# Five input chunks of 512 columns in place of seven, with other spacings between the parts of attention

## The chip, the core and the metric

The kernel runs on one NeuronCore of a Trainium2 chip. The metric is the device time of one launch in microseconds; three runs of the kernel before gave 290.32, 290.36 and 291.07, median 290.36. TensorE (PE in the profile) multiplies, VectorE (DVE), ScalarE (ACT) and GpSimd (POOL) work elementwise, and SyncE (SP) starts the loads.

## The reference

Two layers of a hybrid attention block on 256 tokens of width 1024. Each layer normalizes x, projects it to ten groups of columns, runs three kinds of attention with a gate on each, and adds the output projection to x:

```python
def hybrid_layer(x, mem, norm_g, w_in, w_out, mem_norm_g, w_mem_kv, qk_g):
    h = rms_norm(x, norm_g)
    proj = jnp.einsum('btd,de->bte', h, w_in)
    ...
    a_q, a_k, a_v, a_g, b_q, b_k, b_v, b_g, m_q, m_g = jnp.split(proj, cuts, axis=-1)
    qa = rope(rms_norm(to_heads(a_q, N_HEADS_MOBA), qk_g[0]))
    ...
    oa = from_heads(moba_attention(qa, ka, to_heads(a_v, N_HEADS_MOBA)))
    ...
    ob = from_heads(dilated_attention(qb, kb, to_heads(b_v, N_HEADS_DIL)))
    ...
    om = from_heads(memory_attention(qm, km, to_heads(m_v, N_HEADS_MEM)))
    y = jnp.concatenate([oa * jax.nn.silu(a_g), ob * jax.nn.silu(b_g), om * jax.nn.silu(m_g)], axis=-1)
    return x + jnp.einsum('bte,ed->btd', y, w_out)
```

The groups aq, ak, av, ag, bq, bk, bv and bg have 384 columns each (six heads of 64), mq and mg 256 (four heads). Queries and keys get a norm for each head, those of a and b a rotation as well. With 256 tokens the a heads are causal attention, the b heads causal attention with a fixed bias for each distance, and the m heads look at a second input, mem, without a mask.

## The kernel before

Weights come from memory in units of up to 1 MB and are cut into a high and a low part: ScalarE casts `hi` (L467), VectorE subtracts to `lo` (L468). Normalized x stands transposed as `xmh` and `xml`, cut in the same way, and each product is three matmuls: high by high, low by high, high by low. TensorE thus has three matmuls for each of the 8 slices k of the width and each of 2 row tiles of 128 tokens.

A layer goes through its columns in chunks. For queries, keys and values a chunk is a projection with x as the weights of the array and the chunk's columns moving (`project`), into two accumulators, one PSUM bank for each row tile. In before the chunks are mkv (512, from mem), mq (256), then bq, bk, bv, aq, ak, av with 384 columns each. The gates mg, bg0, bg1, ag0, ag1 are computed transposed with 256 tokens moving (`project_t`), whatever their width. There are four accumulator banks (`acc`), so a chunk's second accumulator waits until the last reader of an earlier chunk is through: the norms of queries and keys (`normed`, VectorE with help of ScalarE and GpSimd) or, for a gate, a tanh `th` on ScalarE and a product `gate` on VectorE (`gates`).

Attention goes by pairs of heads, numbered by the 128 rows of the output that they make: e = 0 to 2 are the a heads, 3 to 5 the b heads, 6 and 7 the m heads. A pair is a Python generator (`pair_of_heads`): four transposes of queries and keys into a bank `wk` (there are three), a copy `qkT` by ScalarE, scores, a maximum `nm` on VectorE, an exponential and a normalization on ScalarE (`pr`), transposes of the probabilities, a copy `pT` on ScalarE, products with the values (`o<-pT,v`), and the gated result `y` on VectorE, which ScalarE casts to the high part of `yT` and VectorE subtracts to its low part.

TensorE works through its instructions in the order in which the program was written out. That order is made by a clock in the program text: `mm` advances `clock[0]` by what a matmul should take, and after each step of a chunk `poll` runs the generators that have become due. A generator says with `yield D_...` how far behind the present step its next one shall stand. So the constants D_* on top of the file place the parts of attention among the products of the chunks; `finish` advances the clock until a pair is through. A queue on another engine has its own order, the one that a scheduler gave the instructions, and is also worked through from first to last.

The output projection takes the rows of `yT` in the order e = 6, 7, 3, 4, 5, 0 into four banks; e = 1 and 2 come last, by bank: three banks for e = 1, the same for e = 2, then the fourth bank for both.

Of the kernel before, what the change touches and what calls it, by code (L numbers as in the profile page):

```python
# [16 lines left out]
P = 128  # L17
T = 256
# [9 lines left out]
PR_BUFS = 3  # L28
# [39 lines left out]
def hybrid_kernel(ctx: ExitStack, tc: tile.TileContext, x, mem, mem_t, gains, w_in, w_out, w_mem_kv, qk_g, const, out):  # L68
# [26 lines left out]
    mem_sb = cp.tile([P, NT, D], F32, name="mem_sb")  # L95
# [174 lines left out]
    def normed(accs, n, dsts, tables, scale=None):  # L270

        h = n // HD
        half = dict(s=2, d=HD // 2)
        held = []
        for t, acc in enumerate(accs):
# [3 lines left out]
            first = tables[0][t][:, None, :].to_broadcast([P, h, HD])  # L279
            if scale is None:  # L280
                pin(nc.vector.tensor_tensor(heads(t1), heads(acc), first, op=ALU.mult))
            else:
                pin(nc.vector.scalar_tensor_tensor(heads(t1), heads(acc), scale, first, op0=ALU.mult, op1=ALU.mult))
            if len(tables) > 1:
                pin(nc.vector.tensor_tensor(t2.rearrange("p (h s d) -> p h s d", **half),
                                            acc.rearrange("p (h s d) -> p h s d", **half)[:, :, ::-1, :],
                                            tables[1][t].rearrange("p (s d) -> p s d", s=2)[:, None]
                                            .to_broadcast([P, h, 2, HD // 2]), op=ALU.mult))
            held.append((t1, t2, rs))

        def rest():
            for (t1, t2, rs), dst in zip(held, dsts):
                if len(tables) > 1:
                    pin(nc.vector.tensor_tensor(t1, t1, t2, op=ALU.add))
                pin(nc.vector.tensor_tensor(heads(dst), heads(t1), rs.unsqueeze(2).to_broadcast([P, h, HD]),
                                            op=ALU.mult))
# [3 lines left out]
    live = dict(pr=0, pT=0, o=0, heads=0, pairs=0, s=0, t=0, v=0)  # L300

    def pair_of_heads(qn, kn, pair, masks, v, gate, ready, finished, alone):
# [10 lines left out]
        yield from until(lambda: live["s"] == me and live["pr"] + 2 <= PR_BUFS)  # L313
# [3 lines left out]
        live["pr"] += 2  # L317
        scores = [work() for _ in range(2)]
# [8 lines left out]
        for j in range(2):  # L327
            rest = head(2 * me + j, scores[j], spans, masks, pTs, D_SOFTMAX - 1.5 * alone)
            spawn(rest, next(rest))
        yield D_SOFTMAX - 1.5 * alone  # L330
# [409 lines left out]
```

## Time and profile before

| | us |
|---|---|
| median of three runs | 290.36 |
| profiled execution | 289.94 |
| its span, first to last instruction | 288.1 |
| outside the span | 1.84 |
| TensorE busy (98%) | 282.3 |
| VectorE busy (71%) | 205.9 |
| ScalarE busy (69%) | 199.0 |
| GpSimd busy (19%) | 53.4 |
| mean granted clock of TensorE | 1.000 (2.4 GHz) |

A share of busy time close to 100% says that an engine hardly stands, not that it works at its peak. What bounds a kernel is read from the chain of work that ended last and from the waits on it. A row of a timeline gives the start from the span's beginning, the time for which the group of equal instructions lasted, how many there were (x; here one matmul of single precision is sometimes two records) and, in brackets, how long the engine had stood before and what it waited for.

### The profile page before, as it was taken

What the parts mean: (1) busy time and instruction counts of PE and PEld (TensorE: products, weight loads), DVE (VectorE), ACT (ScalarE), POOL (GpSimd) and SP (SyncE); (2) the same over time, 40 slices, a digit from 0 to 9 for tenths busy, and PEclk for the clock granted to TensorE, in tenths of its full rate; (3) what the DMA queues carried; (4) which work ended last, traced back from release to release, by engine and by line L of the source; (5) the groups of instructions that cost most, each with busy time, mean ns of one, the idle gap of its engine ahead of it and who ended that gap; (6) DMA issues with size and microseconds to landing.
All of it is one profiled execution on the core that took longest, in us unless ns stands there. A gap on an engine that the chain in (4) does not pass through costs nothing.

```text
span 288.1 us, 4967 instructions
## 1 busy us (share of the span) xinstructions
PE 282.3 (98%) x1810; PEld 250.5 (87%) x1810; DVE 205.9 (71%) x461; ACT 199.0 (69%) x446; POOL 53.4 (19%) x72
## 2 busy tenths in 40 slices
PE   6999999999999999999999999999999999999994
PEld 5799999898989998777788999989898989897773
DVE  1798999794659987754686576979755899655423
ACT  3899678877678779688267554868685778777620
POOL 0103993200003300000020079403000312000000
PEclk9999999999999999999999999999999999999999
DMA  7999675527430656528024918360845443820003
GB/s 246 390 367 369 207 220 161 170 55 273 111 109 17 206 171 262 190 109 290 1 91 168 275 54 236 131 175 9 281 115 154 146 132 96 361 73 0 3 0 146
DMA packets 32793, 47.33 MB, mean 164 GB/s; under 512 B 1280, under 2 KB 27648, under 8 KB 32768
## 3 DMA queue, kind: packets, MB, share of 16 engines
q1 hardware_dynamic: 32336, 46.22, 48.7%
q10 hardware_dynamic: 432, 0.79, 0.9%
q8 instruction: 14, 0.23, 0.3%
q14 instruction: 11, 0.09, 0.1%
HBM read 45.96 MB, written 1.05 MB: 163 GB/s over the span
## 4 chain that ended last, share of the span: by engine, by line
PE 97%; DMA 1%; DVE 0%; SPq 0%; DVEq 0%; issue 0%
PE acc L111 79%; PE wk L114 8%; PE wk L111 5%; PE o L111 5%; DMA memT<-in_mem_t_dram 1%; PE o L114 0%; DVE x_sb L706 0%; SPq L487 0%; DVE whole L533 0%; DVEq L736 0%; DVEq L533 0%
## 5 line engine op out<-in xcount | busy, mean ns | idle before, releaser
L468 DVE TENSOR_TENSOR lo<-raw,hi 128x768 fp32r<-128x768 f32 (+1 forms) x90 | 95.3, 1087 | 20.4 <-ACT hi L467 19.3
L467 ACT CAST hi<-raw 128x768 fp32r<-128x768 f32 (+1 forms) x90 | 82.5, 937 | 26.8 <-PE acc L111 16.9
L111 PE MATMUL acc<-hi,xmh 128*128 128x384 f32 (+2 forms) x252 | 66.6, 346 | 0.0
L111 PE MATMUL acc<-lo,xmh 128*128 128x384 f32 (+2 forms) x252 | 63.7, 335 | 0.0
L111 PE MATMUL acc<-hi,xml 128*128 128x384 f32 (+2 forms) x252 | 63.6, 334 | 0.0
L156 POOL TENSOR_TENSOR hrs<-ms,mhalf 128x6 f32<-128x6 f32 (+1 forms) x24 | 29.9, 1248 | 116.0 <-DVE ms L155 115.7
L111 PEld LDWEIGHTS acc<-hi,xmh 128*128 128x128 f32 x252 | 43.0, 189 | 4.1 <-issue 2.2
L111 PEld LDWEIGHTS acc<-lo,xmh 128*128 128x128 f32 x252 | 45.0, 188 | 1.1
L111 PEld LDWEIGHTS acc<-hi,xml 128*128 128x128 f32 x252 | 44.9, 188 | 1.1
L111 PE MATMUL acc<-hi,yT 128*128 128x512 f32 x128 | 40.9, 401 | 0.0
L111 PE MATMUL acc<-xmh,hi 128*128 128x256 f32 x128 | 29.7, 293 | 0.0
L378 ACT ACTIVATE pr<-pr,nm 128x128 f32<-128x128 f32 (+1 forms) x48 | 21.3, 445 | 12.0 <-DVE nm L376 12.0
L111 PE MATMUL acc<-xmh,lo 128*128 128x256 f32 x128 | 28.4, 283 | 0.0
L111 PE MATMUL acc<-xml,hi 128*128 128x256 f32 x128 | 28.3, 283 | 0.0
L111 PEld LDWEIGHTS acc<-hi,yT 128*128 128x128 f32 x128 | 23.0, 188 | 4.8 <-issue 0.7
L384 ACT ACTIVATE pr<-pr,rinv 128x128 f32<-128x128 f32 (+1 forms) x64 | 25.5, 461 | 0.0
L111 PE MATMUL acc<-lo,yT 128*128 128x512 f32 x64 | 25.1, 391 | 0.0
L111 PEld LDWEIGHTS acc<-xml,hi 128*128 128x128 f32 x128 | 21.0, 191 | 0.0
L111 PEld LDWEIGHTS acc<-xmh,lo 128*128 128x128 f32 x128 | 21.0, 191 | 0.0
L111 PEld LDWEIGHTS acc<-xmh,hi 128*128 128x128 f32 x128 | 20.9, 191 | 0.0
L376 DVE CUSTOM_DVE_ANT_0 pr<-wk,cst 128x128 f32<-128x128 f32 (+1 forms) x48 | 14.3, 353 | 8.6 <-PE wk L111 8.3
L395 ACT COPY pT<-wk 128x384 f32<-128x384 f32 (+1 forms) x32 | 15.2, 508 | 7.2 <-PE wk L114 7.1
(83 smaller groups left out, 354.6 us busy)
## 6 DMA issues: line engine op xcount, KB each, us to landing
raw<-in_w_in_dram SPq DMA_DIRECT2D x24, 768.0 KB, 5.5
raw<-in_w_in_dram SPq DMA_DIRECT2D x7, 1024.0 KB, 6.6
raw<-in_w_out_dram SPq DMA_DIRECT2D x6, 1024.0 KB, 4.9
raw<-in_w_in_dram SPq DMA_DIRECT2D x6, 512.0 KB, 4.1
raw<-in_w_out_dram SPq DMA_DIRECT2D x4, 512.0 KB, 4.2
raw<-in_w_mem_kv_dram SPq DMA_DIRECT2D x2, 1024.0 KB, 5.7
raw<-in_w_mem_kv_dram SPq DMA_DIRECT2D x2, 512.0 KB, 6.7
x_sb<-in_x_dram SPq DMA_DIRECT2D x2, 512.0 KB, 6.4
```

Source lines behind the costliest of these rows:

```text
L111: pe(nc.tensor.matmul(out, a, b, start=start, stop=stop), us)
L114: pe(nc.tensor.transpose(out, a, ident), 0.109)
L156: pin(nc.gpsimd.tensor_tensor(dst, ms, mhalf[:, :n], op=ALU.pow))
L376: nc.vector.tensor_tensor_reduce(out=pr[:, spans[t]], in0=s[:, spans[t]], in1=masks[t], scale=-1.0, scalar=3e38, op0=ALU.add, op1=ALU.min, ...
L378: nc.scalar.activation(pr[:, spans[t]], pr[:, spans[t]], AF.Exp, scale=-1.0, bias=nm[:, t:t + 1], accum_out=sums[:, t:t + 1])
L384: nc.scalar.activation(pr[:, spans[t]], pr[:, spans[t]], AF.Copy, scale=rinv[:, t:t + 1])
L395: nc.scalar.copy(pT[:, :n], ps[:, :n])
L467: pin(nc.scalar.copy(hi, raw))
L468: pin(nc.vector.tensor_tensor(lo, raw, hi.bitcast(F32), op=ALU.subtract))
```

## The change

Queries, keys and values are cut anew: c0 = mq and the last 256 columns of bv, c1 = bq and the first 128 of bk, c2 = the rest of bk, the first 128 of aq, the first 128 of bv, c3 = the rest of aq and the first 256 of ak, c4 = the rest of ak and av. All have 512 columns, the gates stay. The order of a layer is mkv, c0, mg, c1, c2, bg0, bg1, c3, c4, ag0, ag1 and the output projection. A load of a chunk that consists of several ranges of columns is one DMA for each. `normed` takes the columns in spans that have tables of their own, and queries and keys of a kind stand in a common tile `qk`. The constants of the spacings change, the shorter ones for the last pair (e = 2, `alone`) are dropped, pairs 3, 5 and 7 get longer ones, and there are four buffers of probabilities in place of three. The copy of mem, `mem_sb`, takes the buffer of the first raw weights.

```diff
-PR_BUFS = 3
+PR_BUFS = 4
...
-D_NORM, D_MEM, D_QK, D_SOFTMAX, D_PT, D_EVAC = 8, 1, 2.5, 5, 2.5, 4
+D_NORM, D_WIDE, D_MEM, D_QK, D_SOFTMAX, D_PT, D_EVAC = 8, 9.5, 6.5, 2.5, 5, 2.5, 4
...
-D_PARTNER, D_SCORES = 5, 14
+D_BUSY, D_SCORED = 1.5, 4
+D_PARTNER, D_SCORES = 8, 14
...
-    def normed(accs, n, dsts, tables, scale=None):
+    def normed(accs, n, spans, outs, scale=None):
...
-        yield from until(lambda: live["s"] == me and live["pr"] + 2 <= PR_BUFS)
+        yield from until(lambda: live["s"] == me and live["pr"] + 2 <= PR_BUFS and clock[0] >= live["next"])
...
+        live["next"] = clock[0] + D_SCORED
...
-        yield D_SOFTMAX - 1.5 * alone
+        yield D_SOFTMAX + D_BUSY * busy
         yield from until(lambda: len(pTs) == 2)
-        yield D_PT - alone
+        yield D_PT
...
+    for name, pieces in (("c0", (("mq", 0, 256), ("bv", 128, 384))), ("mg", (("mg", 0, 256),)),
+                         ("c1", (("bq", 0, 512),)), ("c2", (("bk", 128, 384), ("aq", 0, 128), ("bv", 0, 128))),
+                         ("bg0", (("bg", 0, 256),)), ("bg1", (("bg", 256, 384),)),
+                         ("c3", (("aq", 128, 640),)), ("c4", (("ak", 256, 768),)),
+                         ("ag0", (("ag", 0, 256),)), ("ag1", (("ag", 256, 384),))):
+        in_cols[name] = [(first_col[c] + lo, first_col[c] + hi) for c, lo, hi in pieces]
...
-        order += [(l, c) for c in ["mkv", "mq", "mg", "bq", "bk", "bv", "bg0", "bg1", "aq", "ak", "av", "ag0", "ag1", "om", "ob", "oa"]]
+        order += [(l, c) for c in ["mkv", "c0", "mg", "c1", "c2", "bg0", "bg1", "c3", "c4", "ag0", "ag1", "om", "ob", "oa"]]
...
+    mem_sb = sp.tile([P, NT, D], F32, tag="yT0", name="mem_sb", bufs=1)
...
-            ahead[0] = SPLIT_BUFS - 2
+            ahead[0] = SPLIT_BUFS - 1
...
+        accs = run(project(xs, weights(), 512))
+        normed(accs, 512, [span(0, 384, 2), span(384, 512, 3)], [(0, 512, by_tile(qk, 0, 512))])()
+        start_heads(range(1), 3, qn, kn, masks, v, gate, ready, D_WIDE)
+        accs = run(project(xs, weights(), 512))
+        normed([acc[:, 0:384] for acc in accs], 384, [span(0, 256, 3), span(256, 384, 0)],
+               [(0, 256, by_tile(qk, 512, 768)), (256, 384, by_tile(qk_a, 0, 128))])()
+        for t, acc in enumerate(accs):
+            nc.scalar.copy(v[:, t, 0:128], acc[:, 384:512])
+        start_heads(range(1, 3), 3, qn, kn, masks, v, gate, ready)
```

What the constants do is seen in the order of the instructions. The first place is TensorE at the end of layer 1, from the last products with values (pair e = 2) on; `yT` is the gated result, a wait in brackets is on ScalarE's cast or VectorE's subtraction. Before, the pair's two last values products and what follows them (the first wait is for e = 1, the second for e = 2):

```order
L111 MATMUL o<-pT,v 64x128 x2
L111 MATMUL acc<-hi,yT_1952 128x512 [waits Activation_49]
L111 MATMUL acc<-hi,yT_1953 128x512 [waits DVE_49]
L111 MATMUL acc<-lo,yT_1952 128x512
L111 MATMUL acc<-hi,yT_1952 128x512
L111 MATMUL acc<-hi,yT_1953 128x512
L111 MATMUL acc<-lo,yT_1952 128x512
L111 MATMUL acc<-hi,yT_1952 128x512
L111 MATMUL acc<-hi,yT_1953 128x512
L111 MATMUL acc<-lo,yT_1952 128x512
L111 MATMUL acc<-hi,yT_1952 128x512 [waits Activation_49]
L111 MATMUL acc<-hi,yT_1953 128x512 [waits DVE_49]
```

And of the change, the product ahead of them, the values products of e = 2, and what follows (the waits are for e = 2):

```order
L111 MATMUL acc<-hi,yT_1843 128x512
L111 MATMUL acc<-lo,yT_1842 128x512
L111 MATMUL o<-pT,v 64x256 [waits PE_49]
L111 MATMUL o<-pT,v 64x256
L111 MATMUL o<-pT,v 64x128 x2
L111 MATMUL acc<-hi,yT_1842 128x512 [waits Activation_49]
L111 MATMUL acc<-hi,yT_1843 128x512 [waits DVE_49]
L111 MATMUL acc<-lo,yT_1842 128x512
```

The nine products of e = 1 for three banks stood behind the last values, and now stand ahead of them; 24 products follow the values before, 15 now.

The second place is VectorE in layer 0 between mg and the chunk behind it, up to the second gate of mg; t, qn, kn and mqn belong to the norms of the memory heads, hss and ms to the sums of squares. Before:

```order
L295 TENSOR_TENSOR qn<-t_340,hrs 128x256
L295 TENSOR_TENSOR qn<-t_350,hrs 128x256
L632 SCALAR_TENSOR_TENSOR t_392<-v,rmem,gB 128x256
L468 TENSOR_TENSOR lo<-raw,hi 128x768
L635 TENSOR_TENSOR kn<-t_392,hrs 128x256
L632 SCALAR_TENSOR_TENSOR t_395<-v,rmem,gB 128x256
L582 SCALAR_TENSOR_TENSOR gate<-th,acc 128x256
L635 TENSOR_TENSOR kn<-t_395,hrs 128x256
L582 SCALAR_TENSOR_TENSOR gate<-th,acc 128x256
```

Of the change:

```order
L287 SCALAR_TENSOR_TENSOR t_394<-acc,gB 128x256
L262 TENSOR_REDUCE hss<-sq 128x4
L595 SCALAR_TENSOR_TENSOR gate<-th,acc 128x256
L155 TENSOR_SCALAR ms<-hss 128x4
L287 SCALAR_TENSOR_TENSOR t_404<-acc,gB 128x256
L301 TENSOR_TENSOR mqn<-t_394,hrs 128x256
L301 TENSOR_TENSOR mqn<-t_404,hrs 128x256
L480 TENSOR_TENSOR lo<-raw,hi 128x1024
L595 SCALAR_TENSOR_TENSOR gate<-th,acc 128x256
```

The first gate, which frees the bank that the second accumulator of c1 takes, stands ahead of the norm of c0's second row tile; the norm of the memory keys has moved further up, out of these rows.

The third place is ScalarE in layer 0 between the last softmax ahead of ag0's tanh and ag1's tanh (th). Before:

```order
L384 ACTIVATE pr<-pr,rinv 128x128
L384 ACTIVATE pr<-pr,rinv 128x256
L593 CAST yT_257<-y 128x256
L581 ACTIVATE th<-acc 128x256 x2
L467 CAST hi<-raw 128x1024
L395 COPY pT<-wk 128x384
L581 ACTIVATE th<-acc 128x256
L467 CAST hi<-raw 128x1024
L395 COPY pT<-wk 128x384
```

Of the change, from ag0's tanh to ag1's:

```order
L594 ACTIVATE th<-acc 128x256 x2
L386 ACTIVATE pr,sums<-pr,nm 128x128
L316 COPY qkT<-wk 128x512
L386 ACTIVATE pr,sums<-pr,nm 128x256
L386 ACTIVATE pr,sums<-pr,nm 128x128
L392 ACTIVATE pr<-pr,rinv 128x128
L392 ACTIVATE pr<-pr,rinv 128x256
L386 ACTIVATE pr,sums<-pr,nm 128x256
L609 CAST yT_258<-y 128x256
L392 ACTIVATE pr<-pr,rinv 128x128
L392 ACTIVATE pr<-pr,rinv 128x256
L594 ACTIVATE th<-acc 128x256
```

The softmax of a pair (e = 0), with its copy of queries and keys and a cast of `yT`, stands between the two.

## Rows read from the trace of the kernel before

**Rows 1.** page of the profile, busy time of each engine
```profile
PE 282.3 (98%) x1810; PEld 250.5 (87%) x1810; DVE 205.9 (71%) x461; ACT 199.0 (69%) x446; POOL 53.4 (19%) x72
```

**Rows 2.** page of the profile, chain that ended last, by engine
```profile
PE 97%; DMA 1%; DVE 0%; SPq 0%; DVEq 0%; issue 0%
```

**Rows 3.** waits of TensorE, all that the view names
```profile
PE acc L111 <- DVE whole L533: 1.1, 1, 1.1
PE warm L121 <- DVE mhalf L84: 1.0, 1, 1.0
```

**Rows 4.** timeline of TensorE, layer 0, mg to bq (start, duration in us)
```profile
30.33 0.40 PE L111 MATMUL acc<-xmh,lo 128*128 128x256 f32 x2
30.57 0.52 PE L111 MATMUL acc<-hi,xmh 128*128 128x384 f32 x2
...
35.78 0.27 PE L114 MATMUL wk<-ident,qn 128*128 128x128 f32 x1
```

**Rows 5.** timeline of TensorE, end of layer 1
```profile
277.91 0.87 PE L111 MATMUL o<-pT,v 128*64 128x256 f32 x8
278.71 0.74 PE L111 MATMUL acc<-hi,yT 128*128 128x512 f32 x2
...
280.91 0.63 PE L111 MATMUL acc<-hi,yT 128*128 128x512 f32 x2
...
283.64 0.62 PE L111 MATMUL acc<-hi,yT 128*128 128x512 f32 x2
```

**Rows 6.** timeline of ScalarE, layer 0, gates of mg and of bg1
```profile
30.65 0.66 ACT L581 ACTIVATE th<-acc 128x256 f32<-128x256 f32 x2 [0.41 <-PE acc L111]
...
74.48 0.39 ACT L581 ACTIVATE th<-acc 128x256 f32<-128x256 f32 x1
```

**Rows 7.** timeline of VectorE, layer 0, gate of bg1
```profile
74.90 0.42 DVE L582 SCALAR_TENSOR_TENSOR gate<-th,acc 128x256 f32<-128x256 f32 x1 [1.10 <-ACT th L581]
```

**Rows 8.** timeline of VectorE, layer 0, five splits, then norms of a chunk
```profile
59.52 5.22 DVE L468 TENSOR_TENSOR lo<-raw,hi 128x1024 fp32r<-128x1024 f32 x5
...
86.03 0.55 DVE L262 TENSOR_REDUCE hss<-sq 128x6 f32<-128x384 f32 x1
...
90.83 0.95 DVE L468 TENSOR_TENSOR lo<-raw,hi 128x768 fp32r<-128x768 f32 x1
```

**Rows 9.** timeline of TensorE, layer 0, scores to third output bank
```profile
108.47 0.93 PE L111 MATMUL wk<-qkT 64*128 64x128 f32 x8
...
110.13 0.33 PE L114 MATMUL wk<-ident,qn 128*128 128x128 f32 x1
...
119.12 0.62 PE L111 MATMUL acc<-hi,yT 128*128 128x512 f32 x2
```

**Rows 10.** timeline of ScalarE, layer 0, softmax of that pair
```profile
110.34 0.40 ACT L378 ACTIVATE pr<-pr,nm 128x128 f32<-128x128 f32 x1 [0.56 <-DVE nm L376]
...
112.58 1.04 ACT L467 CAST hi<-raw 128x1024 fp32r<-128x1024 f32 x1
113.53 1.49 ACT L384 ACTIVATE pr<-pr,rinv 128x128 f32<-128x128 f32 x4
114.93 0.39 ACT L593 CAST yT<-y 128x256 fp32r<-128x256 f32 x1
```

**Rows 11.** timeline of VectorE, layer 0, first maximum of that pair
```profile
110.02 0.28 DVE L376 CUSTOM_DVE_ANT_0 pr<-wk,cst 128x128 f32<-128x128 f32 x1
```

**Rows 12.** timeline of VectorE, end of layer 1
```profile
278.83 0.42 DVE L359 SCALAR_TENSOR_TENSOR y<-o,gate 128x256 f32<-128x256 f32 x1 [2.29 <-PE o L111]
279.73 0.42 DVE L594 TENSOR_TENSOR yT<-y,yT 128x256 fp32r<-128x256 f32 x1 [0.47 <-ACT yT L593]
```

**Rows 13.** timeline of ScalarE, end of layer 1
```profile
279.29 0.41 ACT L593 CAST yT<-y 128x256 fp32r<-128x256 f32 x1 [3.21 <-DVE y L359]
```

**Rows 14.** timeline of TensorE, transposes of probabilities
```profile
75.32 0.49 PE L114 MATMUL wk<-ident,pr 128*128 128x128 f32 x3
```

**Rows 15.** timeline of ScalarE, copy of those transposes
```profile
75.84 0.48 ACT L395 COPY pT<-wk 128x384 f32<-128x384 f32 x1 [0.26 <-PE wk L114]
```

More of the change, by code (lines that the diff above doesn't have):

```diff
@@ L287, in normed @@
+            for a, b, tables in spans if rotated else ():
+                pin(nc.vector.tensor_tensor(t2[:, a:b].rearrange("p (h s d) -> p h s d", **half),
+                                            acc[:, a:b].rearrange("p (h s d) -> p h s d", **half)[:, :, ::-1, :],
                                             tables[1][t].rearrange("p (s d) -> p s d", s=2)[:, None]
[L288 removed]
+                                            .to_broadcast([P, (b - a) // HD, 2, HD // 2]), op=ALU.mult))
@@ L297, in normed, with pair_of_heads @@
         return rest
     pending = {}
-    live = dict(pr=0, pT=0, o=0, heads=0, pairs=0, s=0, t=0, v=0)
-    def pair_of_heads(qn, kn, pair, masks, v, gate, ready, finished, alone):
+    live = dict(next=0, pr=0, pT=0, o=0, heads=0, pairs=0, s=0, t=0, v=0)
+    def pair_of_heads(qn, kn, pair, masks, v, gate, ready, finished, alone, busy):
         ps = work()
@@ L416, in hybrid_kernel @@
         else:
-            n = 512 if c == "mkv" else in_cols[c][1]
+            n = 512 if c == "mkv" else sum(hi - lo for lo, hi in in_cols[c])
             nk = 8 if n <= 256 else 4
@@ L640, in hybrid_kernel @@
+            if i == 3 and l:
+                normed(keys, 256, [(0, 256, [[gB[:, l, 5]] * NT])], [(0, 256, keys)])()
+        for t, acc in enumerate(accs):
+            pin(nc.scalar.copy(v_b[:, t, 128:384], acc[:, 256:512]))
+        normed([acc[:, 0:256] for acc in accs], 256, [(0, 256, [[gB[:, l, 4]] * NT])], [(0, 256, by_tile(qn, 0, 256))],
+               0.125)()
+        ahead[0] = SPLIT_BUFS - 1
         pinning[0] = False
-        start_heads(2, 6, qn, kn, None, v, gate, ready, D_NORM + D_MEM)
+        start_heads(range(2), 6, qn, kn, None, v, gate, ready, D_MEM)
@@ L642, in hybrid_kernel, with span @@
         tab = prepare_tables(l)
+        def span(a, b, kind):
+            return a, b, [[tab[:, kind, c, t] for t in range(NT)] for c in range(2)]
         gates(run(project_t(xs, weights(), 256)), gate)
@@ new lines, in hybrid_kernel @@
+        for t, acc in enumerate(accs):
+            nc.scalar.copy(v[:, t, 0:128], acc[:, 384:512])
+        start_heads(range(1, 3), 3, qn, kn, masks, v, gate, ready)
+        ready["v"] = clock[0] + D_EVAC
+        gates(run(project_t(xs, weights(), 256)), gate[:, 0:2])
+        gates(run(project_t(xs, weights(), 128)), gate[:, 2:3])
+        masks = [cst[:, C_CAUSAL + 128:C_CAUSAL + 256], cst[:, C_CAUSAL:C_CAUSAL + 256]]
+        if l + 1 < DEPTH:
+            mem_xs = xm_tiles()
+            spawn(next_mem(mem_xs, gT[:, 24 + 8 * l:32 + 8 * l]), D_FIRST_MEM)
@@ new lines, in hybrid_kernel @@
+        (v, gate), qk = head_tiles(384, 384), qk_a
+        qn, kn = qk[:, :, 0:384], qk[:, :, 384:768]
+        ready = dict(v=1e9)
+        accs = run(project(xs, weights(), 512))
+        normed(accs, 512, [span(0, 256, 0), span(256, 512, 1)], [(0, 512, by_tile(qk, 128, 640))])()
+        start_heads(range(2), 0, qn, kn, masks, v, gate, ready, D_WIDE)
+        accs = run(project(xs, weights(), 512))
+        normed([acc[:, 0:128] for acc in accs], 128, [span(0, 128, 1)], [(0, 128, by_tile(qk, 640, 768))])()
@@ L671, in hybrid_kernel @@
+        for t, acc in enumerate(accs):
+            nc.scalar.copy(v[:, t], acc[:, 128:512])
+        start_heads(range(2, 3), 0, qn, kn, masks, v, gate, ready)
+        ready["v"] = clock[0] + D_EVAC
+        gates(run(project_t(xs, weights(), 256)), gate[:, 0:2])
+        gates(run(project_t(xs, weights(), 128)), gate[:, 2:3])
         whole_banks = [(t, c, 512) for t in range(NT) for c in (0, 512)]
```

149 lines of the change are left out of this document (65 added, 84 removed).

## The prediction

> **What bounds the kernel now.** I read the busy shares first, then the chain that ended last, then TensorE's waits, and only then the timelines of the places that the change touches. TensorE is busy for 282.3 of 288.1 us [rows 1], the chain consists of TensorE for 97% of the span [rows 2], and the view of TensorE's waits names one wait of 1.1 us before a product and otherwise only the one before the warming matmuls [rows 3]. So there is no stage in which another engine ends last: the time is the sum of what TensorE issues, and VectorE and ScalarE matter only where a matmul stands behind one of their results. Two things can move the time: how long TensorE takes for its list, and every new wait in that list, which is paid in full.
>
> **What the list itself gains.** The time of a matmul here is its columns plus a fixed part. From the start of the last 256-column group to that of the first 384-column one two matmuls take 0.24 us, 0.120 each; from 30.57 to 35.78 us thirty 384-column matmuls take 5.21, 0.1737 each [rows 4]; at the layer's end twelve 512-column ones take 2.73 us, 0.2275 each [rows 5]. At 2.4 columns per ns the columns alone are 0.1067, 0.160 and 0.2133, so about 13.3 ns stay with each matmul whatever its width. Per k, row tile and product the old chunks need one 256 and six 384, the new ones five 512: the same 2560 columns in two matmuls fewer. With 8 k, 2 row tiles, 3 products and 2 layers that is 96 places and 192 matmuls fewer, 192 x 13.3 ns = **-2.56 us**. TensorE has no cover, so all of it counts, and so does each wait below: all of TensorE's list stands behind a matmul that waits, while ScalarE and VectorE only catch up. The bounds of the gain are 2.4 (with 0.2275 for the wide ones and 0.1737 for the others, 96 x (0.120 + 6 x 0.1737 - 5 x 0.2275)) and 2.6.
>
> The Trainium skill, page "TensorE: Matmul & The Clock Gate", section "Wait — 56ns, not 53.3ns?", puts the fixed part of a matmul at the full clock at about 2.5 ns. The rows here do not agree, they show five times that; by the page the gain would be 192 x 2.5 ns = 0.48 us and the sum below would come to 295.2.
>
> **The start of c1 in layer 0.** The second accumulator of c1 is the PSUM bank in which the first half of mg stood. It is free when the gate operation on VectorE has read it, which follows the tanh on ScalarE. From the start of mg's last pair of matmuls to the start of the tanh are 0.32 us (30.33 to 30.65) [rows 4, 6]; a tanh that stands alone starts 0.42 before its gate, and the gate takes 0.42 [rows 6, 7]. So the bank is free 1.16 us after the start of that pair, while TensorE wants it after 0.24 + 0.23 = 0.47: **+0.7**. In layer 0 of before, the bank that comes next was freed by the mq chunk's norm. The bounds are 0.5 (a tanh of 0.33, as in a pair of them that takes 0.66) and 1.1 (VectorE is a split late). In layer 1 the banks stand the other way round and I see no wait.
>
> **The start of c3 in both layers.** The second accumulator of c3 waits for bg0's first gate in the same way. On VectorE the gate stands behind c2's norms, the first dilated pair's maxima and two splits; on ScalarE its tanh stands behind that pair's exponentials. The norms of a 384-wide chunk take 4.8 us (86.03 to 90.83) and a split of 1024 about 1.0 (five in 5.22) [rows 8]. Behind c2's last matmul I count, as an estimate, 0.9 for the squares, 4.8 + 0.3 for the norms with their additional spans, 0.3 for the first maximum, 1.8 for the exponentials, 0.3 for a cast, 1.4 for the four normalizations, 0.84 for tanh and gate: 10.6. TensorE has 72 matmuls of 0.12, scores and values of a pair, eight transposes and one wide matmul in between, about 12. That is no wait if VectorE is abreast when c2 ends, and 1.5 per layer if it enters two to three splits late, as c1's norms and five splits in a row can make it. I take the lower half, 0.2 per layer: **+0.4**.
>
> **The start of the output projection in both layers.** Its third bank is that of ag1. In before only a cast and a copy stood between ag0's tanh and ag1's; the rows of the order show it now behind the whole softmax of the first causal pair, whose scores TensorE issues four transposes and eighteen narrow products ahead of ag1's end. In before that softmax took, from the scores' start at 108.47 to the end of the normalizations at 114.93, 6.46 us [rows 9, 10], with the maxima starting 1.55 behind the scores [rows 11]; 0.95 of it was a cast of weights (112.58 to 113.53) that now is elsewhere. So 5.5, then a cast of 0.3 and 0.84 for tanh and gate: 6.6 to 6.7 behind the scores. TensorE wants the bank after scores and values (1.66, 108.47 to 110.13), four transposes (0.4), 18 x 0.12 and 9 x 0.2275: 6.3. So 0.35 is the lower bound, and with VectorE's four splits and two gates ahead of the maxima it goes up to 1.9. Before had 10.65 us for the same (108.47 to 119.12). I take 0.7 per layer, nearer the lower end: **+1.4**.
>
> **The end of each layer.** This is where I am surest. The delays that were shorter for the last pair (e = 2) have become the ordinary ones. In before 24 products followed that pair's values, and the first nine of them needed only e = 1. Now its values stand nine products later, and the next matmul needs e = 2 itself. In the rows the values start at 277.91 and the next product at 278.71; the pair's y starts at 278.83, the cast ends at 279.70, the subtraction at 280.15 [rows 5, 12, 13]. Behind the start of the values that is 0.80 for TensorE against 1.79 for the first product's operand and 2.24 for the second's: a wait of 0.99 and another 0.22, together 1.2. The nine products for e = 1 (2.05 us) covered it; now nothing does. Pair e = 1 gets a smaller wait: between its values and its first product there are three transposes and three products, 0.80 + 0.3 + 0.68 = 1.8, while its cast stands behind the copy of the last transposes, which starts 0.52 behind them (75.32 to 75.84) and holds ScalarE for 0.38 [rows 14, 15]. That gives 0.80 + 0.52 + 0.38 + 0.41 = 2.11 for the cast and 2.56 for the subtraction: 0.3 and 0.2. I take 1.6 of 1.7 per layer: **+3.2**, with bounds of 2.4 (the smaller wait is hidden) and 3.5.
>
> **What costs nothing.** Splits become 20 of 1024 per layer instead of 24 of 768 and 2 of 1024; both engines have slack of over 80 us. The norms get seven VectorE operations more per layer and row tile pair, about 1 us, covered by the same slack except in front of c3, where it is counted. Three more loads on SP's queue and c2's pieces of 128 columns reach the splits ahead of their use by some 2 us as I estimate; without that cover a late piece would stop TensorE. The fourth buffer of probabilities takes a wait away and adds none. The memory's rows now load behind the first weights' last use; they are needed some 10 us later.
>
> **The sum.** 289.94 - 2.56 + 0.7 + 0.4 + 1.4 + 3.2 = **293.1 us**, against the profiled execution (span 288.1 and 1.84 around it). The median of the runs, 290.36, is 0.4 above it, less than the terms are uncertain by, so I leave the number.
>
> **Rivals.** (a) The gain comes through. The waits at the layer's ends need the last pair's values to stand where the order has them, but if TensorE in before also loses small amounts at the busy pairs' transposes (a listing of its matmuls at the row's prices is 1.4 us short of the trace, spread thinly), the later transposes give that back: 289.94 - 2.56 - 1.4 + 2.4 = 288.4, faster, if none of the bank waits is there. For it speaks the thin loss; against it that the view of TensorE's waits names nothing there [rows 3]. It decides from 0.4 us given back on, since gain and waits for e = 2 alone leave 289.8. (b) Gains and waits cancel: only the two waits for e = 2 and that of c1 are real, 289.94 - 2.56 + 2.4 + 0.7 = 290.5, no change. For it speaks that all else is a walk through queues; against it that the walk puts each at over zero. (c) VectorE falls behind by the upper bounds in front of c3 and of the output projection: 293.1 + 2.6 + 2.4 = 298.1 with everything, 295 to 296 with half. For it speaks that c2's norms now stand next to five splits. (d) The late piece of c2: each us of delay in its two halves is a us of time, 294 to 296. (e) The page's fixed part of 2.5 ns: 295.2; the rows of three widths speak against it.
>
> **How the numbers follow.** About 0.3% (0.9 us) is what a measurement of this kernel can tell from no change. As summed, 291.5 to 294.7: 0.52. (a) 0.14. (b) 0.17. (c), (d) and (e) together 0.17, (e) 0.01 of it. The range leaves out most of (a) and what is over 295.7: 288.8 to 295.7. Faster 0.14, same 0.17, slower 0.69.
>
> **What would show it.** The products of the profile after should have 192 matmuls less in the chunks, at 0.2275 each. TensorE should stand for about 1 us behind the last values of each layer, released by ScalarE's cast, and for 0.7 at the start of c1, released by VectorE's gate; at the output projection a wait of a half to one and a half us should be released by the third gate. The prediction is wrong if TensorE's busy share stays at 98% (then (a)), or if the wait behind e = 2 is under 0.5 us. VectorE without idle time from c1's end to c3 would speak for (c), a split released by a load of c2 for (d).

## The result and the profile after

The changed kernel takes 298.5 us (median of four runs, 298.21 to 299.5), the kernel before 290.72 in the same comparison (four runs, 290.32 to 291.33). The ratio is 1.0287, with an interval of 1.0258 to 1.0316: slower by 7.8 us. The direction is the one forecast; the time is 5.4 us over the forecast and 2.8 us beyond the end of its range. The profiled execution took 298.41 us with a span of 296.4, 8.3 longer than that of before.

Of the page of the changed kernel, the busy time of each engine and the chain that ended last answer to [rows 1, 2]:

```profile
PE 285.1 (96%) x1618; PEld 228.2 (77%) x1618; DVE 206.6 (70%) x477; ACT 198.0 (67%) x438; POOL 54.8 (18%) x72
...
PE 73%; ACT 10%; DMA 7%; DVE 7%; issue 2%; POOL 1%; SPq 0%; DVEq 0%; ACTq 0%; POOLq 0%
```

TensorE issues the 192 matmuls fewer that were counted (1810 to 1618), yet its busy time has grown by 2.8 us: a part of the time for which a matmul waits counts as busy, as the prices below show. Its share of the chain has gone from 97% to 73%, since the chain now passes through ScalarE, VectorE and a load wherever TensorE stands. Where it stands, the view of its waits says (total us, times, longest), to be held against [rows 3]:

```profile
PE acc L111 <- DVE gate L595: 3.2, 4, 1.2
PE acc L111 <- ACT yT L609: 2.3, 4, 1.0
...
PE acc L111 <- ACT th L594: 0.4, 1, 0.4
```

These are the three kinds of place that the prediction named: a product that waits for a gate's bank, a product of the output projection that waits for `yT`, and the start of c1. The timeline of TensorE (start, duration, and in brackets the wait) shows one of each kind, in this order: c1 in layer 0, the first product behind c2 there (no wait), c3 in layer 0, the third bank of the output projection in layer 0, c3 in layer 1, and the end of layer 1:

```profile
35.87 0.40 PE L111 MATMUL acc<-xmh,lo 128*128 128x256 f32 x2
36.70 1.06 PE L111 MATMUL acc<-hi,xmh 128*128 128x512 f32 x2 [0.43 <-ACT th L594]
...
65.96 0.40 PE L111 MATMUL acc<-xmh,hi 128*128 128x256 f32 x2
...
77.42 0.48 PE L111 MATMUL acc<-hi,xmh 128*128 128x512 f32 x1
79.06 0.50 PE L111 MATMUL acc<-hi,xmh 128*128 128x512 f32 x1 [1.15 <-DVE gate L595]
...
120.30 0.39 PE L111 MATMUL acc<-lo,yT 128*128 128x512 f32 x1
121.56 0.72 PE L111 MATMUL acc<-hi,yT 128*128 128x512 f32 x2 [0.87 <-DVE gate L595]
122.12 0.40 PE L111 MATMUL acc<-lo,yT 128*128 128x512 f32 x1
...
220.13 0.48 PE L111 MATMUL acc<-hi,xmh 128*128 128x512 f32 x1
221.08 0.50 PE L111 MATMUL acc<-hi,xmh 128*128 128x512 f32 x1 [0.46 <-DVE gate L595]
...
283.60 0.40 PE L111 MATMUL acc<-lo,yT 128*128 128x512 f32 x1
284.17 0.96 PE L111 MATMUL acc<-hi,yT 128*128 128x512 f32 x2 [0.18 <-ACT yT L609]
284.97 0.39 PE L111 MATMUL acc<-lo,yT 128*128 128x512 f32 x1
...
286.67 0.87 PE L111 MATMUL o<-pT,v 128*64 128x256 f32 x8
288.51 0.96 PE L111 MATMUL acc<-hi,yT 128*128 128x512 f32 x2 [0.96 <-ACT yT L609]
289.31 0.40 PE L111 MATMUL acc<-lo,yT 128*128 128x512 f32 x1
```

The price of a place is the time from one start to the next minus the pace there. It is larger than the bracket, since the bracket counts from the end of the record before, and a record of 0.48 is followed by the next start after 0.23 where nothing waits. At c3 in layer 0 one wide matmul is followed after 1.64 us (77.42 to 79.06): 1.4 paid, of which the bracket names 1.15. Behind the values of e = 2 the pace is that of the same place in before, 0.80 to the first product [rows 5] and 0.58 from there (278.71) to the third, which has this row:

```profile
279.29 0.40 PE L111 MATMUL acc<-lo,yT 128*128 128x512 f32 x1
```

Worked out in this way: c1 1.0 (0.59 from 35.87 to 36.70, where 0.24 is the pace, and 0.44 in the pair that starts there, 1.06 long where 0.62 is usual); c3 1.4 in layer 0 and 0.7 in layer 1; the third bank of the output projection 1.1 and 0.9 (in layer 0 1.03 in front of the pair at 121.56 and 0.11 in it); the layers' ends 1.95 each, namely 0.34 and 0.35 for the two operands of e = 1 (283.60 and 284.17, where 0.23 and 0.45 are the pace) and 1.04 and 0.22 for those of e = 2 (286.67 to 288.51 and 288.51 to 289.31). Together 1.0 + 2.1 + 2.1 + 3.9 = 9.1 us, against 5.7 in the forecast's sum; the view of the waits names 3.2 + 2.3 + 0.4 = 5.9 of them.

Why c3's price is so much larger than forecast stands in VectorE's and ScalarE's timelines ahead of it. First VectorE of the changed kernel, layer 0:

```profile
55.62 0.69 DVE L262 TENSOR_REDUCE hss<-sq 128x8 f32<-128x512 f32 x1 [2.88 <-ACT sq L260]
...
64.95 3.48 DVE L480 TENSOR_TENSOR lo<-raw,hi 128x1024 fp32r<-128x1024 f32 x3
68.36 0.54 DVE L262 TENSOR_REDUCE hss<-sq 128x6 f32<-128x384 f32 x1
...
73.56 0.28 DVE L384 CUSTOM_DVE_ANT_0 pr<-wk,cst 128x128 f32<-128x128 f32 x1
...
78.58 0.75 DVE L595 SCALAR_TENSOR_TENSOR gate<-th,acc 128x256 f32<-128x256 f32 x2 [0.33 <-ACT th L594]
```

Then ScalarE of the same kernel, layer 0 and, in the last row, layer 1:

```profile
66.66 0.86 ACT L260 ACTIVATE sq<-acc 128x384 f32<-128x384 f32 x2
...
73.78 1.05 ACT L479 CAST hi<-raw 128x1024 fp32r<-128x1024 f32 x1 [1.68 <-PE acc L111]
74.73 0.40 ACT L386 ACTIVATE pr<-pr,nm 128x128 f32<-128x128 f32 x1
...
76.79 1.49 ACT L392 ACTIVATE pr<-pr,rinv 128x128 f32<-128x128 f32 x4
78.19 0.62 ACT L594 ACTIVATE th<-acc 128x256 f32<-128x256 f32 x2
...
219.50 0.80 ACT L392 ACTIVATE pr<-pr,rinv 128x128 f32<-128x128 f32 x2
```

Both squares of c2 are done at 67.52, the first about 67.1. VectorE takes up the reduction at 68.36 because three splits in a row stand ahead of it; it ends the norms and starts the first maximum at 73.56. The norms took 5.2 us, close to the estimate of 5.1 (4.8 + 0.3); VectorE came to them late. The first maximum is done at 73.84, but ScalarE has a cast of weights in its queue ahead of the exponentials, which start only at 74.73: another 0.9, which the forecast's walk does not have. Then come the exponentials, a cast and four normalizations, the tanh (78.19) and the gate (78.58, done about 79.0). TensorE wanted the bank at 77.65.

Counted from 65.96, when TensorE leaves c2, the gate is done after 13.0 instead of 10.6. Of this VectorE's queue has 1.6 (the first maximum 7.6 behind instead of 6.0) and the cast 0.9; TensorE itself comes after 11.7 instead of 12. In layer 1 VectorE and the cast are as late (the first maximum starts 3.84 ahead of c3, 3.86 in layer 0), but the tanh stands behind two of the normalizations (the row at 219.50) and not behind four: this is the difference between 1.4 and 0.7.

### The profile page after: what moved, and what is told of

Read it like the earlier page. It is cut to its first block, busy times and chain, and to the rows that moved or that the text cites. A ratio compares the mean times of both kernels' runs of the same rounds, so it can differ in the third digit from the quotient of the medians.

```text
span 296.4 us, 4600 instructions
## 1 busy us (share of the span) xinstructions
PE 285.1 (96%) x1618; PEld 228.2 (77%) x1618; DVE 206.6 (70%) x477; ACT 198.0 (67%) x438; POOL 54.8 (18%) x72
## 4 chain that ended last, share of the span: by engine, by line
PE 73%; ACT 10%; DMA 7%; DVE 7%; issue 2%; POOL 1%; SPq 0%; DVEq 0%; ACTq 0%; POOLq 0%
PE acc L111 59%; PE wk L114 6%; PE wk L111 4%; PE o L111 4%; DMA raw<-in_w_in_dram 4%; DVE lo L480 3%; ACT pr L386 3%; DMA x_sb<-in_x_dram 2%; ACT pr L392 2%; ACT hi L479 2%; DVE gate L595 1%; ACT yT L609 1%; DMA raw<-in_w_mem_kv_dram 1%; ACT qkT L316 1%; POOL hrs L156 0%
## 5 line engine op out<-in xcount | busy, mean ns | idle before, releaser
L480 DVE TENSOR_TENSOR lo<-raw,hi 128x1024 fp32r<-128x1024 f32 x78 | 94.0, 1224 | 21.3 <-ACT hi L479 20.6
L479 ACT CAST hi<-raw 128x1024 fp32r<-128x1024 f32 x78 | 81.1, 1054 | 30.3 <-PE acc L111 26.9
L111 PE MATMUL acc<-hi,xmh 128*128 128x512 f32 x188 | 62.5, 414 | 2.1 <-DVE gate L595 1.6
L111 PE MATMUL acc<-hi,xml 128*128 128x512 f32 x188 | 57.8, 392 | 0.0
L111 PE MATMUL acc<-lo,xmh 128*128 128x512 f32 x188 | 57.6, 391 | 0.0
L156 POOL TENSOR_TENSOR hrs<-ms,mhalf 128x4 f32<-128x4 f32 (+3 forms) x24 | 30.2, 1267 | 129.3 <-DVE ms L155 129.3
L111 PEld LDWEIGHTS acc<-lo,xmh 128*128 128x128 f32 x188 | 35.2, 188 | 8.1 <-DVE lo L480 0.2
L111 PEld LDWEIGHTS acc<-hi,xml 128*128 128x128 f32 x188 | 35.3, 188 | 7.7
L111 PEld LDWEIGHTS acc<-hi,xmh 128*128 128x128 f32 x188 | 32.5, 189 | 9.9 <-DVE gate L595 2.7
L114 PE MATMUL wk<-ident,pr 128*128 128x128 f32 x104 | 16.5, 274 | 0.0
```

Of the source, the lines that this page charges most:

```text
L111: pe(nc.tensor.matmul(out, a, b, start=start, stop=stop), us)
L114: pe(nc.tensor.transpose(out, a, ident), 0.109)
L156: pin(nc.gpsimd.tensor_tensor(dst, ms, mhalf[:, :n], op=ALU.pow))
L479: pin(nc.scalar.copy(hi, raw))
L480: pin(nc.vector.tensor_tensor(lo, raw, hi.bitcast(F32), op=ALU.subtract))
```

## The experiments

The theory (theory 1 in the expectations): each named place is a wait that TensorE pays in full, the places are independent, and so each can be bought back alone. The rival (theory 2): ScalarE and VectorE carry a backlog, so that a wait which is taken away at one place comes out at another. Four kernels of the first comparison, with before at 290.02 us (median of eleven runs), test them. The changed kernel was not measured again there, and before stood 0.7 us higher in its own comparison, so differences to its 298.5 are that uncertain; TensorE's list, from its first product with `xmh` to its last with `yT`, serves beside them. It lasts 275.43 us in before (8.67 to 284.10) and 283.26 in the changed kernel (8.83 to 292.09).

**The last pair's delays.** Against the changed kernel, the shorter delays of the pair e = 2 come back:

```diff
-            rest = head(2 * me + j, scores[j], spans, masks, pTs, D_SOFTMAX + D_BUSY * busy)
+            rest = head(2 * me + j, scores[j], spans, masks, pTs, D_SOFTMAX + D_BUSY * busy - 1.5 * alone)
-        yield D_SOFTMAX + D_BUSY * busy
+        yield D_SOFTMAX + D_BUSY * busy - 1.5 * alone
-        yield D_PT
+        yield D_PT - alone
```

> The changed kernel with the shorter delays for the last pair put back (minus 1.5 at the softmax, minus 1 at the transposes), everything else as changed. Theory 1 (each wait that the trace after shows on TensorE is paid in full and by itself): both waits at each layer's end vanish, that is 0.34 + 0.35 for pair e = 1 and about 1.0 + 0.35 for pair e = 2, about 2.0 per layer, so 298.5 - 4.0 = 294.5. Theory 2 (VectorE and ScalarE are behind in the whole layer, the waits only show where their backlog comes out): the transposes of the last pair, now earlier, wait for its softmax instead, and less than half is gained, 296.5 or more.

294.97 us, ratio to before 1.0175 (1.0151 to 1.0198): 3.5 us less than the changed kernel, and 3.8 less in the list. In TensorE's waits of this kernel the line of `yT` is gone and the gates' line is as it was.

**The chunk's first bank first.** The first two k of a 512-column chunk are issued for row tile 0 and then for row tile 1, so that a chunk's second bank is wanted later:

```diff
+                if k0 == 0 and not pinning[0]:
+                    for t in range(NT):
+                        products([(accs[t], k, [x[:, k, t * P:(t + 1) * P] for x in xs], [p[:, k] for p in w])
+                                  for k in range(nk)], 0, KD - 1)
+                        yield
+                    continue
```

> The changed kernel with one difference: the first two k slices of a chunk of 512 columns go through the first row tile and then through the second, so that the second accumulator of c1 and c3 is wanted 1.1 us later. Theory 1: the waits at the start of c1 in layer 0 (about 1.0) and of c3 (1.4 and 0.7) go but for 0.3 in layer 0 of c3, so 298.5 - 2.8 = 295.7. Theory 2: VectorE is behind between c1's end and c3, so the time taken from the wait for the gate comes back as a wait for c3's second split or for the transposes of the first dilated pair: 297.5 or more.

296.37 us, ratio 1.0214 (1.0196 to 1.0232): 2.1 less, and 3.0 in the list, though this profile starts late (its first product with `xmh` is at 10.79, where after has 8.83). Of its waits, the tanh is gone, the two gates of c3 are gone, and the two of the output projection stay:

```profile
PE acc L111 <- ACT yT L615: 2.3, 4, 1.0
PE acc L111 <- DVE gate L601: 1.8, 2, 1.1
```

**The fourth bank last.** In the output projection's first part, three banks take e = 6 and e = 7 first, and the fourth bank both afterwards, so that the bank of ag1 is wanted later:

```diff
+        mem_w = []
...
+                if c == "om":
+                    mem_w.append((e, w))
+                    for part in whole_banks[:3]:
+                        out_products(e, w, *part)
+                        poll()
+                    for e_m, w_m in mem_w if k == 1 else ():
+                        out_products(e_m, w_m, *whole_banks[3])
+                        poll()
+                    continue
```

> The changed kernel with one difference: in the output projection the two row blocks of the memory heads (e = 6, 7) go through three banks first and through the fourth, that of ag1's gate, after that, so it is wanted 9 matmuls (2.0 us) later. Theory 1: the waits for that gate (1.0 and 0.8) go, so 298.5 - 1.8 = 296.7. Theory 2: ScalarE's softmax of pair e = 0 is what is late, its transposes come next in TensorE's list and wait then: 298.0 or more.

296.76 us, ratio 1.0227 (1.0197 to 1.0258): 1.7 less, and 1.5 in the list, whose start has a wait of 0.4 for `xn` in this profile that the changed kernel's has not. Of the four gates in its waits only c3's two are left:

```profile
PE acc L111 <- DVE gate L595: 1.6, 2, 1.2
```

**All three.**

> The changed kernel with the three differences of the runs beside it together. Theory 1: the sum of the three, 4.0 + 2.8 + 1.8 = 8.6, so 289.9, which is a little under the kernel before and shows the gain of the fewer matmuls less what is left of the waits. Theory 2: backlogs come out elsewhere, 293 or more.

290.82 us, ratio 1.0021 (1.0 to 1.0042): 7.7 less than after, and 8.7 less in the list. Separately the three gave 3.5 + 2.1 + 1.7 = 7.3, in the list 8.3. Nothing came out elsewhere: theory 2 falls. The page's chain and the waits of this kernel read like those of before [rows 2, 3]:

```profile
PE 96%; DMA 1%; DVE 0%; SPq 0%; DVEq 0%; issue 0%
...
PE warm L121 <- DVE mhalf L85: 1.0, 1, 1.0
PE acc L111 <- DVE whole L552: 0.4, 1, 0.4
```

One small wait is left that no bracket names: in layer 0 the two operands of e = 1 still come late, by 0.45 us in all, in and around this pair, 0.96 long where 0.62 is usual (the cast ends at 138.61, the subtraction at 139.06):

```profile
138.66 0.96 PE L111 MATMUL acc<-hi,yT 128*128 128x512 f32 x2
```

With the other waits gone the five chunks should show their gain, and the time does not. Six more kernels ask where it is, and what the edits that were costed at nothing are worth. The first four were compared with before at 290.31 us (seven runs), the last two with before at 290.23 (seventeen runs).

**The last pair's delays taken from the kernel before.** The same edit as the first, the other way round, on the old seven chunks:

```diff
-            rest = head(2 * me + j, scores[j], spans, masks, pTs, D_SOFTMAX - 1.5 * alone)
+            rest = head(2 * me + j, scores[j], spans, masks, pTs, D_SOFTMAX)
-        yield D_SOFTMAX - 1.5 * alone
+        yield D_SOFTMAX
-        yield D_PT - alone
+        yield D_PT
```

> The kernel before with one edit alone: the delays of the last pair, which the change took away, are taken away here with the old seven chunks. Theory 1 (the waits at the layers' ends come from where the last pair's values stand, whatever the chunks are): the same edit was worth 3.5 us in the kernel after, so 290.0 + 3.5 = 293.5 us (292.5 to 294.5), with products of yT that wait for ScalarE's cast of yT twice per layer. Rival (the new chunks leave VectorE and ScalarE so late that the layer's end pays for it): under 1 us, 290.0 to 291.0, since the old chunks leave both engines slack.

292.8 us, ratio 1.0092 (1.0061 to 1.0124): 2.5 more than before, at the lower end of the first theory's range and far above the rival's. Its waits have the one of 0.96 behind e = 2, once per layer:

```profile
PE acc L111 <- ACT yT L593: 1.9, 2, 1.0
```

So about 2.5 of the 3.9 us at the layers' ends belong to where e = 2 stands, twice the 1.04 + 0.22 found above; the small waits for e = 1 come only together with the new chunks' order.

**Each wide product in two halves.** On the kernel with all three edits, all 512-column products of the input chunks and of the memory's keys and values, but the first of each bank, are issued as two of 256 columns, 542 matmuls more:

```diff
-                mm(acc, a, b, start=k == first and i + j == 0, stop=k == last and j == 1)
+                n = acc.shape[-1]
+                begin = k == first and i + j == 0
+                for c in ((0, n),) if x_moves or n < 512 or last != KD - 1 or begin else ((0, 256), (256, 512)):
+                    mm(acc[:, c[0]:c[1]], a, b[:, c[0]:c[1]], start=begin, stop=k == last and j == 1 and c[1] == n)
```

> The kernel with all three edits, in which every 512-column product of an input chunk but the first of each bank is issued as two of 256 columns: the same columns in 542 matmuls more (2 x 5 x 46 in the chunks, 36 and 46 for the memory's keys and values). It measures what a matmul costs beside its columns. The prediction's 13.3 ns whatever the width: 290.8 + 7.2 = 298.0. The pace between starts in the trace after (0.120 for 256 columns, 0.2305 for 512, so 9.5 ns for the additional one): 290.8 + 5.1 = 295.9. The Trainium skill's 2.5 ns (page 'TensorE: Matmul & The Clock Gate', section 'Wait - 56ns, not 53.3ns?') would give 292.2.

294.72 us, ratio 1.0157 (1.0123 to 1.0191): 3.9 to 4.4 us above the kernel with all three edits (290.82, and 290.33 in the repetition below). TensorE's list can be compared without its start and its end, from the last `yT` product of layer 0 to that of layer 1. Its timeline in the kernel before, the two rows:

```profile
144.98 0.39 PE L111 MATMUL acc<-lo,yT 128*128 128x512 f32 x1
...
284.10 0.39 PE L111 MATMUL acc<-lo,yT 128*128 128x512 f32 x1
```

with all three edits:

```profile
145.26 0.39 PE L111 MATMUL acc<-lo,yT 128*128 128x512 f32 x1
...
283.53 0.39 PE L111 MATMUL acc<-lo,yT 128*128 128x512 f32 x1
```

and with the halves:

```profile
147.67 0.39 PE L111 MATMUL acc<-lo,yT 128*128 128x512 f32 x1
...
288.64 0.39 PE L111 MATMUL acc<-lo,yT 128*128 128x512 f32 x1
```

The layer takes 139.12 us before, 138.27 with all three edits and 140.97 with the halves. The halves add 276 matmuls in this layer (five chunks and the keys and values, 46 each) and 2.70 us: 9.8 ns for each. The five chunks save 96 matmuls and 0.85 us: 8.9 ns for each. For the whole kernel it is 7.2 to 8.1 ns (3.9 to 4.4 us for 542). All are under the 13.3 ns of the forecast, and none is near the 2.5 ns of the Trainium skill (page "TensorE: Matmul & The Clock Gate", section "Wait — 56ns, not 53.3ns?"), which would have given 0.7 and 0.24 us.

**c2's norm without its rotation.** On the changed kernel; this leaves the rotation of c2's queries and keys out of the computation and thereby six operations of VectorE per layer ahead of c3's start:

```diff
-    def normed(accs, n, spans, outs, scale=None):
+    def normed(accs, n, spans, outs, scale=None, turn=True):
...
-        rotated = len(spans[0][2]) > 1
+        rotated = turn and len(spans[0][2]) > 1
...
-               [(0, 256, by_tile(qk, 512, 768)), (256, 384, by_tile(qk_a, 0, 128))])()
+               [(0, 256, by_tile(qk, 512, 768)), (256, 384, by_tile(qk_a, 0, 128))], turn=False)()
```

> The kernel after without the rotation in c2's norms: four multiplications and two additions of VectorE are left out per layer, 2.2 us of its queue just ahead of c3's start (that part of the computation is missing). Theory 1 (the gate that frees c3's second bank is late because VectorE's queue is): both waits at c3's start vanish (1.15 and 0.46 named, 1.4 and 0.7 by the pace), so 2.1 us less than after, 296.4 where after had 298.5, ratio to before 1.020. Rival (ScalarE's own queue, the four normalizations ahead of the tanh, sets it, or TensorE's transposes do): the waits stay within 0.2 us, 298.2 to 298.6.

296.32 us, ratio 1.0205 (1.0175 to 1.0234): 2.2 less than after (2.3 in the list), as the first theory says. On TensorE both row tiles of c3 start as one pair, without a bracket:

```profile
77.10 0.71 PE L111 MATMUL acc<-hi,xmh 128*128 128x512 f32 x2
```

on VectorE the gates start at 76.78 where after has 78.58:

```profile
72.60 0.28 DVE L384 CUSTOM_DVE_ANT_0 pr<-wk,cst 128x128 f32<-128x128 f32 x1
...
76.78 0.75 DVE L595 SCALAR_TENSOR_TENSOR gate<-th,acc 128x256 f32<-128x256 f32 x2 [0.55 <-ACT th L594]
```

and on ScalarE the exponentials start right behind the maximum:

```profile
72.93 0.40 ACT L386 ACTIVATE pr<-pr,nm 128x128 f32<-128x128 f32 x1 [1.10 <-DVE nm L384]
```

So a maximum that starts 0.96 us earlier brings the gate 1.80 earlier, and only the 0.96 is VectorE's. The other 0.84 is ScalarE's: the order of its queue has changed with the edit, the cast of weights that ran from 73.78 in after no longer stands between maximum and exponentials, and these start 0.33 behind the maximum instead of 1.17. The run thus shows that the two queues together make c3's wait; it does not part them, and no run takes away the cast alone. The rival's number (298.2 to 298.6) falls, its mechanism, ScalarE's own queue, does not.

**The busy pairs without their delay.** On the kernel with all three edits, the busy pairs' transposes go back to where they would stand without the new delay:

```diff
-D_BUSY, D_SCORED = 1.5, 4
+D_BUSY, D_SCORED = 0, 4
```

> The kernel with all three edits, with the busy pairs' additional delay set to zero, so that their transposes stand one to three products earlier again. The prediction's step (it costs nothing and gives nothing back): 290.8 within 0.4, no product or transpose that waits for the probabilities. Rival (a) of the prediction (TensorE loses small amounts at busy pairs and the later transposes give them back): 291.5 to 292.5, with transposes of pr that wait for ScalarE.

298.28 us, ratio 1.0261 (1.0217 to 1.0304): 7.5 us more, and the largest miss among the expectations. The prediction's rival (a) had the delay give back 0.4 or 1.4 us; it keeps away far more. The waits name the transposes of the probabilities:

```profile
PE wk L114 <- ACT pr L398: 3.7, 4, 1.8
```

The rest is partly TensorE's clock. After the longest of these waits the timeline has 256-column products 0.21 us apart (219.88 to 220.09), and the windows of 2 us (their start and end, length, busy times, then the granted clock, the DMA share and GB/s) show why:

```profile
216.00:218.00 2.00, 0.98 (x9) 0.74 (x7) 2.00 (x6) 2.00 (x9) 0.00 (x0) 1.00 0.17 66
218.00:220.00 2.00, 1.15 (x5) 0.96 (x6) 1.85 (x5) 2.00 (x9) 0.00 (x0) 0.78 0.01 2
220.00:222.00 2.00, 2.00 (x11) 2.00 (x10) 0.18 (x1) 1.37 (x4) 0.00 (x0) 0.50 0.92 284
222.00:224.00 2.00, 2.00 (x14) 1.92 (x14) 0.00 (x0) 1.27 (x3) 0.00 (x0) 0.86 0.73 246
```

TensorE stood for 1.80 us at 217, and the granted clock fell to 0.5 of full speed, 1.2 GHz, before it rose again: (1 - 0.78 + 1 - 0.50 + 1 - 0.86) x 2 = 1.7 us lost on top of the wait. The runs agree: in three of the four the mean granted clock is 0.991 to 0.994 (298.16 to 298.64 us), in the fourth it is 1.0, and this one took 296.87. The bracketed waits and the clock make 5.4 of the 7.5; the rest was not traced further.

**Three buffers of probabilities.** On the kernel with all three edits:

```diff
-PR_BUFS = 4
+PR_BUFS = 3
```

> The kernel with all three edits and three buffers of probabilities instead of four. A pair's scores then stand a k or more later where the third buffer is still held by the pair before. The prediction's step (the fourth buffer takes a wait away and adds none): 290.8 to 291.5, with no wait of a transpose for ScalarE's probabilities over 0.3 us, if the planner's delays still cover the softmax. Rival (the three-buffer order brings the transposes ahead of the probabilities, as the run without the busy delay did): 292 to 296, with waits for pr of 0.5 us and more.

297.85 us, ratio 1.0259 (1.0233 to 1.0284): 7.5 more than the repetition below, the rival's way and 1.9 beyond its range. The waits that it names are there, and larger ones at the layers' ends, 5.0 us in these two lines; that both come from scores which stand later was not traced further:

```profile
PE acc L111 <- ACT yT L615: 3.1, 4, 1.0
PE wk L114 <- ACT pr L398: 1.9, 3, 0.8
```

**All three once more.**

> The kernel with all three edits once more, to see where the 1 us that its TensorE list is shorter than before's goes. If the long last stores of its first profile (4.98 us where before has 3.26) were chance: a span of about 287.6 in a profile with stores of 3.3, and a median 0.3 to 1.0 us under before's. If the start and the end of this version are longer as a rule: a median 0.3 to 1.0 us over before's again, and 4.5 us or more of stores, or a later first product.

290.33 us (twelve runs), ratio 1.0 (0.9985 to 1.0016): no difference to before. This profile has stores of 3.27 us, so the long ones were chance. Its layer 1 again takes 138.27 us (146.29 to 284.56), 0.85 less than before's, and its layer 0 is longer. The first product with `xmh` is at 8.31, and the last `yT` product of layer 0 at 146.29: 137.98 us, where before has 136.31 (8.67 to 144.98) and the first profile of this version 136.29 (8.97 to 145.26). Its waits show a part of that, in two lines that have no counterpart in [rows 3]:

```profile
PE wk L114 <- DVE xn L528: 0.6, 1, 0.6
...
PE acc L111 <- DVE t L293: 0.2, 1, 0.2
```

The wait for `xn` stands in the five profiles whose first product starts at 8.31 or earlier, and in none of the seven where it starts at 8.67 or later: an early start is lost again there.

## Why the prediction was right or wrong

**Right: the direction, the places and their releasers.** TensorE's list is what is paid. Each of the places of the forecast shows a wait, at the product named, and no other place in the chunks or the output projection does; the three edits, which take away these waits but for 0.45, bring the kernel back to before's time. The waits for e = 2 were worked out as 0.99 and 0.22 and came as 1.04 and 0.22. Of the releasers one needs care: the view puts c1's wait down to the tanh (done at 36.58), but VectorE's norm of c0's first row tile was done within 0.02 of it, and where the run with the fourth bank last waits at this product, the view names this norm. It does not set the price: the second accumulator's product, which the forecast meant, starts at 37.27, right behind the gate (done at 37.21).

**Wrong: the gain.** The step that failed is "about 13.3 ns stay with each matmul whatever its width", as a price for the whole list. As the pace of undisturbed products it holds: the medians from start to start are 0.120, 0.173 and 0.227 us at 256, 384 and 512 columns, 13.3, 13.0 and 13.7 ns over the columns. But the three stretches from which it came [rows 4, 5] are favourable ones, and a product that follows a transpose or a score often takes longer, 0.32 instead of 0.23 for a wide one. Counted with all its intervals, each at the matmul that starts it, layer 1's input products take 68.77 us before and 68.36 with all three edits: 0.41 less, where the constant gives 1.28 for 96 matmuls. Over the pace there are 2.30 us in them before, and 2.99 with the wide chunks. With the halves it is less again (2.1), which is why they cost 9.8 ns each and not 13.3. The rest of the layer's 0.85 is in the gates, transposes and scores (0.9 less) and in the output products (0.4 more). Layer 0 gains the same in its input products (0.43) but nothing in the sum (136.31 and 136.29); 0.45 of what it lacks is the wait that is left there, the rest stands in its gates and scores. So the list's gain is 0.87 + 0.45 = 1.3 us, and the changed kernel's own list says the same: 283.26 - 275.43 = 7.8 us more, with 9.1 paid. A gain of 1.3 instead of 2.56 is 1.3 of the miss. Why the wide products have more time over their pace was not traced further.

**Wrong: c3.** The step that failed is "I take the lower half, 0.2 per layer". It measured 1.4 in layer 0 and 0.7 in layer 1, 2.1 for 0.4. The walk left open whether VectorE is abreast when c2 ends, and this was settled by taking the gentle value; VectorE was 1.6 us late. And the walk put at nothing what ScalarE has in its queue between the maximum and the exponentials, a cast of weights, 0.9 us. This is 1.7 of the miss.

**Mis-sized in the same direction.** The layers' ends: 3.9 for 3.2, mostly for e = 1, whose waits were worked out as 0.3 and 0.2 and came as 0.34 and 0.35; and 1.6 of 1.7 had been taken where 1.95 was paid. The output projection: 2.1 for 1.4, inside its bounds of 0.7 to 3.8. c1: 1.0 for 0.7, inside its bounds; VectorE has a sum of squares ahead of the gate. These three add 0.7 + 0.7 + 0.3. With the two steps above that is 4.7 of the 5.4 us. The other 0.7 lies outside the list and was in no term: 0.6 more ahead of its start, behind its end and outside the span, and 0.1 between profile and median.

**The rivals.** (a) falls twice: the bank waits are there, and the busy pairs' delay prevents 7.5 us rather than giving some back. (b) left out waits that are real; its 2.4 for e = 2 alone was right. (c) is a good part of what decided c3 (VectorE's timeline names no idle time from 55.62 to the start of the maxima), but without ScalarE's cast layer 0 would, as an estimate, have paid 0.5 and not 1.4; the output projection came near the middle of its bounds (1.1 and 0.9 between 0.35 and 1.9). (c)'s 298.1 lies next to the result for partly other reasons, since its sum still had the gain of 2.56. (d): no load appears among TensorE's waits in the chunks. (e): the halves speak against the page's fixed part, but the gain that it gave, 0.48, lies nearer to the 1.3 left over than 2.56 does.

**What costs nothing.** "The fourth buffer of probabilities takes a wait away and adds none" holds, as no wait of the changed kernel is put down to it, and hides its size: without it the new order costs 7.5 us. The same goes for the busy pairs' delay. Neither was costed as the cover that it is.

## What to carry to other kernels

Where one engine is the whole chain, walk for every buffer that it will want to what frees it, through the in-order queue of each engine on the way, and count every entry there, also those that have nothing to do with the buffer (here splits on VectorE and a cast of weights on ScalarE). Where such a walk ends between "no wait" and "a wait", look at whether the freeing engine has any idle time in the stretch ahead, and if it has none, take the upper end. A saving that is a small difference between two large counts should be priced with all intervals of each group, the slow ones behind other work too, not with the best stretch of each. And a delay in a planner that shows no wait may be the cover of one: take it away on its own before calling it free.

## What the runs showed of the hardware

A 512-column matmul cut in two costs 9.8 ns more, measured in place in layer 1. Undisturbed, the products here follow each other after 0.120, 0.173 and 0.227 us at 256, 384 and 512 columns, 13.3, 13.0 and 13.7 ns over the columns at 2.4 GHz. In the kernel without the busy pairs' delay TensorE stood for 1.80 us, the granted clock of the windows behind it was 0.78, 0.50 and 0.86, and 1.7 us more were lost; in the changed kernel, with waits of up to 1.15 us, the granted clock is 1.0 throughout.
